# First operand sums on VectorE, first feature stored without its norm, a job clock with other constants, and two buffer slots that change hands, in a decoder-layer kernel

## The chip, the cores and the metric

The kernel runs on one core of a Trainium2 chip. The metric is the device time of one execution in microseconds (us); lower is better. Engines: TensorE (PE, matrix products into PSUM), VectorE (DVE), ScalarE (ACT), GpSimd (POOL) and SyncE (SP, which starts most transfers between HBM and SBUF). Arithmetic is float32; matrix operands are rounded to the fp32r format.

## The reference, cut to what matters

One layer of a hybrid decoder for 1024 prompt tokens and 8 sampled tokens (1032 columns), model width 1024, feed-forward width 2816:

```python
x = x + 0.5 * swiglu(rmsnorm(x, ffn1_norm_g), ffn1_w_in, ffn1_w_out)
mix = token_mix(rmsnorm(x, mix_norm_g), ...)   # window attention (8 heads) and gated DeltaNet (4 heads), then @ w_out_mix
x = x + mix
x = x + 0.5 * swiglu(rmsnorm(x, ffn2_norm_g), ffn2_w_in, ffn2_w_out)
y = rmsnorm(x, final_norm_g)
# swiglu: gate, up = split(x @ w_in); (silu(gate) * up) @ w_out
# rmsnorm: x * rsqrt(mean(x * x) + eps) * g, per token
# DeltaNet per head and chunk of 64 tokens: v_new = u - w @ S; o = qd @ S + qk @ v_new; S = S * gl + kd^T @ v_new
```

## The kernel before

**Products.** Each float32 operand is split into a rounded part (`hi`, ScalarE) and a rest (`lo`, VectorE or GpSimd), and every product is three matmuls: hi·hi, hi·lo, lo·hi (`mm3`, profile lines L325 to L327; `product`, L515 to L517). The columns are cut into three chunks of 344 or into four of 258 (two pairs: p = 0 and 1, l = 0 and 1 within a pair).

**Stages.** First the head of the first FFN: features f = 0 to 3 (`ffn_head`, plain products with operands `xghi`, `xglo`, `phi`, `plo`). Features 4 to 21 are done by a scheme with seven products for eight blocks (`ffn_in`), for which `x_ops` makes seven operands per pair out of four blocks: the sums `t1`, `t2` and two more, and their splits `xhi`, `xlo`; `w_ops` does likewise for the weights. Then `ffn_out`, the mixers (`mix_in`: projections with attention and the DeltaNet scan between them), `mix_out` in two passes, and the second FFN (`ffn_in` from its first feature, and `ffn_out`). In the trace the mixers span about 758 to 1290 us, `mix_out` to 1377.6, the second FFN the rest.

**Norms.** `prepare` does a pair's norm: `squares` adds up the squares, `rstd` sums them over the partitions on TensorE (line L247, output `nv` after a VectorE step), VectorE makes the reciprocal root by ten small instructions on `rsqt` and `rsqy` (`rsqrt`), and scales the identity by it (tile family `t2`, printed `t` in the profile); TensorE spreads that over the partitions by matmuls with `ones` (called the broadcast below: `ps<-t,ones`). Then VectorE scales each 128x258 block `x`, and `x_ops` runs. In the first FFN's head the products take x without its norm, and `evac` multiplies the results in PSUM by `rs`, the broadcast factor, so it must wait for it.

**Order.** The order of TensorE's instructions is the order in which the program issues them. Norms, attention and scan are generators ("jobs"), resumed by `tick` when the program's own clock `now` reaches `job.at`; the clock is a sum of assumed times: `tick` after each triple of matmuls, `book` for every instruction of another engine, `HOP_NS` between two engines. Where a job's small matmuls stand among the products is set by this clock. The other engines' order is chosen by the compiler's scheduler.

**Buffers.** SBUF data lies in 44 slots of 1060 columns. While weights of `ffn_out`, mixers and `mix_out` stream, `WSLOTS` of them belong to the weights: two `raw`, the others `hi`/`lo` pairs. `reserve` and `drop` keep three weights issued. A weight for which no pair is left is loaded to a wide pair of the common slots by `extra`.

## Time and profile before

| | |
|---|---|
| median of 3 runs | 2123.35 us (2121.09 to 2125.12) |
| profiled execution | 2120.43 us, its span 2118.7 us |
| mean granted TensorE clock | 0.962 of full |
| busy time over the span | TensorE 95%, VectorE 56%, ScalarE 32%, GpSimd 28% |

The span runs from the first to the last instruction. A busy TensorE may run at half clock, so its share of busy time says how often it had an instruction, not how fast that went; the granted clock is the other half of that.

### The profile page before, as it was taken

What the parts mean: (1) busy time and instruction counts of PE and PEld (TensorE: products, weight loads), DVE (VectorE), ACT (ScalarE), POOL (GpSimd) and SP (SyncE); (2) the same over time, 40 slices, a digit from 0 to 9 for tenths busy, and PEclk for the clock granted to TensorE, in tenths of its full rate; (3) what the DMA queues carried; (4) which work ended last, traced back from release to release, by engine and by line L of the source; (5) the groups of instructions that cost most, each with busy time, mean ns of one, the idle gap of its engine ahead of it and who ended that gap; (6) DMA issues with size and microseconds to landing.
All of it is one profiled execution on the core that took longest, in us unless ns stands there. A gap on an engine that the chain in (4) does not pass through costs nothing.

```text
span 2118.7 us, 37131 instructions
## 1 busy us (share of the span) xinstructions
PE 2016.0 (95%) x14990; PEld 1964.4 (93%) x14990; DVE 1187.5 (56%) x2634; ACT 673.7 (32%) x1463; POOL 597.4 (28%) x539
## 2 busy tenths in 40 slices
PE   7899999999999999999898988969999999999997
PEld 6899999999999998879788978869999999999997
DVE  7665444446433545786778865775444444464335
ACT  5233323333111324563332422333323333331112
POOL 2544434431000132330211212454444434200003
PEclk8999999999999999998989989979999999999998
DMA  4212222227321221222112261203222222552112
GB/s 149 66 62 94 77 85 72 80 81 283 100 78 51 96 77 45 58 76 64 47 51 54 71 224 57 98 21 99 71 81 81 81 81 79 181 208 78 56 40 81
DMA packets 115293, 187.16 MB, mean 88 GB/s; under 512 B 36080, under 2 KB 67216, under 8 KB 115104
## 3 DMA queue, kind: packets, MB, share of 16 engines
q1 hardware_dynamic: 113360, 178.41, 26.4%
q0 software_dynamic: 1760, 6.37, 0.8%
q8 instruction: 117, 1.92, 0.4%
q14 instruction: 56, 0.46, 0.1%
HBM read 138.77 MB, written 47.02 MB: 88 GB/s over the span
## 4 chain that ended last, share of the span: by engine, by line
PE 77%; DVE 11%; DMA 2%; issue 1%; ACT 1%; SPq 1%; POOL 0%; DVEq 0%; ACTq 0%; POOLq 0%
PE mm L325 11%; PE mm L326 11%; PE mm L327 10%; PE ps L515 9%; PE ps L516 9%; PE ps L517 9%; PE ps L247 5%; PE mm L516 4%; PE mm L515 4%; PE mm L517 4%; DVE conv L89 1%; DVE inv L89 1%; PE ps L252 1%; DVE x L89 1%; DVE xlo L89 1%
## 5 line engine op out<-in xcount | busy, mean ns | idle before, releaser
L515 PE MATMUL ps<-xhi,wop 128*128 128x258 f32 x1600 | 456.2, 285 | 7.0 <-DVE sw L89 2.9
L516 PE MATMUL ps<-xlo,wop 128*128 128x258 f32 x1600 | 454.6, 284 | 5.5 <-DVE xlo L89 5.5
L517 PE MATMUL ps<-xhi,wop 128*128 128x258 f32 x1600 | 454.4, 284 | 0.0
L325 PE MATMUL mm<-hhi,hi 128*128 128x344 f32 x1008 | 322.6, 320 | 0.0
L326 PE MATMUL mm<-hlo,hi 128*128 128x344 f32 x1008 | 322.2, 320 | 0.0
L327 PE MATMUL mm<-hhi,lo 128*128 128x344 f32 x1008 | 322.0, 319 | 0.0
L515 PEld LDWEIGHTS ps<-xhi,wop 128*128 128x128 f32 x1600 | 304.8, 191 | 8.4 <-DVE sw L89 3.7
L516 PEld LDWEIGHTS ps<-xlo,wop 128*128 128x128 f32 x1600 | 305.8, 191 | 6.1 <-DVE xlo L89 6.1
L517 PEld LDWEIGHTS ps<-xhi,wop 128*128 128x128 f32 x1600 | 304.9, 191 | 0.0
L89 DVE TENSOR_TENSOR wop<-r,wop 128x512 fp32r<-128x512 f32 x200 | 156.0, 795 | 196.7 <-ACT wop L89 178.4
L89 DVE SCALAR_TENSOR_TENSOR x<-mm,x 128x344 f32<-128x344 f32 x240 | 123.3, 515 | 220.9 <-PE mm L327 219.5
L516 PE MATMUL mm<-xlo,wop 128*128 128x258 f32 x640 | 182.2, 285 | 9.0 <-DVE xlo L89 9.0
L327 PEld LDWEIGHTS mm<-hhi,lo 128*128 128x128 f32 x1008 | 189.5, 188 | 0.0
L326 PEld LDWEIGHTS mm<-hlo,hi 128*128 128x128 f32 x1008 | 189.4, 188 | 0.0
L325 PEld LDWEIGHTS mm<-hhi,hi 128*128 128x128 f32 x1008 | 189.3, 188 | 0.0
L89 ACT CAST hi<-raw 128x1024 fp32r<-128x1024 f32 (+2 forms) x79 | 76.2, 965 | 336.3 <-PE mm L326 302.6
L515 PE MATMUL mm<-xhi,wop 128*128 128x258 f32 x640 | 182.0, 284 | 0.0
L517 PE MATMUL mm<-xhi,wop 128*128 128x258 f32 x640 | 181.7, 284 | 0.0
L89 POOL TENSOR_TENSOR acc<-acc,t 128x344 f32<-128x344 f32 (+1 forms) x50 | 47.1, 942 | 473.9 <-ACT t L89 464.2
L89 ACT CAST wop<-r 128x512 fp32r<-128x512 f32 x200 | 120.6, 620 | 181.5 <-DMA r<-in_w_in 132.5
L325 PE MATMUL mm<-xnhi,hi 128*128 128x344 f32 x488 | 173.0, 355 | 0.0
L89 POOL TENSOR_TENSOR ws<-r 128x512 f32<-128x512 f32 x40 | 52.3, 1307 | 402.4 <-DMA r<-in_w_in 375.4
(341 smaller groups left out, 4406.1 us busy)
## 6 DMA issues: line engine op xcount, KB each, us to landing
r<-in_w_in SPq DMA_DIRECT2D x86, 512.0 KB, 3.6
hraw<-hd SPq DMA_DIRECT2D x44, 516.0 KB, 4.9
hd<-sw SPq DMA_DIRECT2D x80, 258.0 KB, 2.0
raw<-in_w_out SPq DMA_DIRECT2D x32, 512.0 KB, 3.7
raw<-in_w_mix SPq DMA_DIRECT2D x22, 512.0 KB, 3.7
x<-in_x SPq DMA_DIRECT2D x16, 516.0 KB, 8.9
raw<-in_w_out SPq DMA_DIRECT2D x20, 384.0 KB, 3.2
xd<-x SPq DMA_DIRECT2D x24, 172.0 KB, 1.9
```

What stands on the lines that cost most here:

```text
L89: return fn(out, *a, **k)
L247: self.nc.tensor.matmul(out, lhsT, rhs, start=start, stop=stop, skip_group_check=pair is not None)
L252: self.nc.tensor.transpose(out, x, self.ident[:p, :p])
L325: mm(ps, whi, xhi, start=start, stop=False)
L326: mm(ps, whi, xlo, start=False, stop=False)
L327: mm(ps, wlo, xhi, start=False, stop=stop)
L515: mm(ps, w[:, a], x[0][:, c], start=first, stop=False, skip_group_check=True)
L516: mm(ps, w[:, a], x[1][:, c], start=False, stop=False, skip_group_check=True)
L517: mm(ps, wlo, x[0][:, c], start=False, stop=last, skip_group_check=True)
```

## The change

1. `WSLOTS` goes from 8 to 6, and two weights instead of three are kept issued (`LIVE`); the two slots return to the common ones. In the last group of each `ffn_out` and in `mix_out`'s last pass two weights instead of one go to wide pairs.
2. The job clock's constants are others: longer ways between engines, a short one for two instructions of one job on one engine, other times for triples of matmuls and for small matmuls; a job that yields `None` is resumed up to 1.2 us of its clock ahead of its being ready.
3. The first feature f = 0 leaves PSUM by eight ScalarE copies into two tiles `early`; when all four `rs` blocks are there, two VectorE multiplications of 128x1032, one Silu, one GpSimd multiplication and one transfer do what 8 VectorE, 4 ScalarE and 4 GpSimd instructions and four transfers did.
4. The four sums of `x_ops` and the sum in `squares` move from GpSimd to VectorE, but for the first FFN's pair 1. In all 12 sums of 128x1032 and two adds of squares move.
5. In `mix_out` the eight additions of squares that VectorE had go to GpSimd.

```diff
-WSLOTS = 8
+WSLOTS = 6
+LIVE = 2
...
-PE_NS = 150.0
-HOP_NS = 130.0
+PE_NS = 220.0
+LEAD = 1200.0
+SELF_HOP = 70.0
...
-        self.vector = Timed(net, nc.vector, 70.0, 1.04)
-        self.scalar = Timed(net, nc.scalar, 95.0, 0.83)
-        self.gpsimd = Timed(net, nc.gpsimd, 150.0, 2.1)
+        self.vector = Timed(net, nc.vector, 65.0, 1.05, 260.0)
+        self.scalar = Timed(net, nc.scalar, 185.0, 0.83, 200.0)
+        self.gpsimd = Timed(net, nc.gpsimd, 150.0, 2.1, 260.0)
...
     def book(self, eng, ns, parts):
         cur = self.cur
-        ready = max(cur.ready, self.now + PE_NS)
+        ready = max(cur.last[1] + SELF_HOP if cur.last[0] is eng else cur.ready, self.now + PE_NS)
...
-        cur.ready = end + HOP_NS
+        cur.last = eng, end
+        cur.ready = end + eng.hop
...
                     lat = next(job.gen)
-                    job.at = self.now - lat if lat < 0 else max(job.ready, self.now) + lat
+                    if lat is None:
+                        job.at = max(job.ready - LEAD, self.now)
+                    else:
+                        job.at = self.now - lat if lat < 0 else max(job.ready, self.now) + lat
...
-        self.now += 15.0 if pair else max(110.0, n * 4 / 2.4)
+        self.now += 15.0 if pair else max(222.0 if lhsT.shape[0] == P else 60.0, n * 4 / 2.4)
...
-        for _ in range(3):
+        for _ in range(LIVE):
             self.issue()
...
-        while self.plan and self.live < 3:
+        while self.plan and self.live < LIVE:
             self.issue()
...
-        self.tick(int(xhi.shape[1]) * 3 / 2.36)
+        self.tick(27.0 + int(xhi.shape[1]) * 1.29)
...
-    def x_ops(self, blk, n, out, keep=0):
-
-        tt = self.nc.gpsimd.tensor_tensor
+    def x_ops(self, blk, n, out, keep, eng):
+
+        tt = eng.tensor_tensor
...
-            self.tick(HW * 3 / 2.2)
+            self.tick(27.0 + HW * 1.29)
...
+        def first():
+            while len(done) < 4:
+                yield -300.0
+            for t in early:
+                nc.vector.tensor_tensor(t, t, rs, ALU.mult)
+            nc.scalar.activation(early[0], early[0], AF.Silu)
+            nc.gpsimd.tensor_tensor(early[1], early[1], early[0], ALU.mult)
+            nc.sync.dma_start(hd[:, 0, :], early[1])
+            self.fr(*early)
+            yield PAD
+
+        early = [self.bt(s="early") for _ in range(2)]
...
-                self.due.append((lambda p=p, l=l: (p, l) in done, partial(evac, f, c, *ps)))
-                self.settle_rs(2 if f == 0 else 1)
+                if f:
+                    self.due.append((lambda p=p, l=l: (p, l) in done, partial(evac, f, c, *ps)))
+                    self.settle_rs(1)
+                else:
+                    for t, o in zip(early, ps):
+                        nc.scalar.copy(t[:, c * HW:(c + 1) * HW], o)
...
-                wide = [(self.bt([P, per * g * P], F32R, "whi"), self.bt([P, per * g * P], F32R, "wlo")) for _ in range(KT // per - 3)]
-                ws = [self.take() for _ in range(3)]
+                wide = [(self.bt([P, per * g * P], F32R, "whi"), self.bt([P, per * g * P], F32R, "wlo")) for _ in range(KT // per - LIVE)]
+                ws = [self.take() for _ in range(LIVE)]
...
-            nc.gpsimd.tensor_tensor(a, a, b, ALU.add)
+            eng.tensor_tensor(a, a, b, ALU.add)
...
                 nc.vector.scalar_tensor_tensor(y, y, self.norm_g[:, gi, k:k + 1], bcs[:, :w], ALU.mult, ALU.mult)
+                yield None
...
-            yield -300.0 if ok else -500.0
+            yield None if ok else -500.0
...
-                last = [self.bt([P, per * g * P], F32R, n) for n in ("whi", "wlo")]
-                ws = [self.take() for _ in range(KT // per - 1)]
-                ws.append(self.extra(*last))
+                wide = [(self.bt([P, per * g * P], F32R, "whi"), self.bt([P, per * g * P], F32R, "wlo")) for _ in range(KT // per - LIVE)]
+                ws = [self.take() for _ in range(LIVE)]
+                for t in wide:
+                    ws.append(self.extra(*t))
...
-                        self.square(acc[:, c % 2 * HW:(c % 2 + 1) * HW], m, at(m, c))
+                        self.square(acc[:, c % 2 * HW:(c % 2 + 1) * HW], m, at(m, c), dve=())
...
-            n.spawn(n.prepare(p, xs[p], n.bt(s="acc"), 0, xT[p], rs, done, xg["ready"]))
+            n.spawn(n.prepare(p, xs[p], n.bt(s="acc"), 0, xT[p], (n.nc.vector, n.nc.gpsimd)[p], rs, done, xg["ready"]))
...
-            n.spawn(n.prepare(p, x, acc, 2, xT[p]))
+            n.spawn(n.prepare(p, x, acc, 2, xT[p], n.nc.vector))
```

In TensorE's and VectorE's order this gives the following. Names are those of the program, with numbers.

TensorE in the head of the first FFN, before: the sums of squares of pair 0 (`ps_55`) and its first broadcast (`ps_60`) stand directly behind one another.

```order
L326 MATMUL mm_54_387<-xglo_29_176,phi_10_109 128x258
L327 MATMUL mm_54_387<-xghi_28_175,plo_11_110 128x258
L247 MATMUL ps_55_436<-ones_76,acc_33_180 86x1 x6
L247 MATMUL ps_60_462<-t2_59_458,ones_76 128x86 x3
L325 MATMUL ps_64_486<-xghi_26_173,phi_3_92 128x258
L326 MATMUL ps_64_486<-xglo_27_174,phi_3_92 128x258
```

After, the broadcast (`ps_66`) has 30 product matmuls between itself and the sums; here is where it stands.

```order
L332 MATMUL ps_64_522<-xglo_17_164,phi_38_185 128x258
L333 MATMUL ps_64_522<-xghi_16_163,plo_39_186 128x258
L253 MATMUL ps_66_527<-t2_63_489,ones_76 128x86 x3
L331 MATMUL ps_64_522<-xghi_16_163,phi_38_185 128x258
L332 MATMUL ps_64_522<-xglo_17_164,phi_38_185 128x258
```

Counted in product matmuls from pair 0's first broadcast, pair 1's sums stood 42 behind it, pair 0's second broadcast 48 and pair 1's first 75; after, they stand 81, 84 and 105 behind it, and the last of the three takes the factors `t2_82`.

VectorE at pair 1's norm in the first FFN's head, before: `t2_70` is that broadcast's input, and the two rows ahead of the last are a feature's `evac`, which waits for `rs_32`.

```order
L89 SCALAR_TENSOR_TENSOR x_6_102<-x_6_102,c_norm_g_74,ps_71_562 128x258 x2
L89 SCALAR_TENSOR_TENSOR x_8_106<-x_8_106,c_norm_g_74,ps_71_562 128x258 x4
L89 TENSOR_TENSOR rsqt_69_540<-rsqy_68_539 86x6
L89 SCALAR_TENSOR_TENSOR rsqt_69_540<-rsqt_69_540,nv_67_531 86x6
L89 SCALAR_TENSOR_TENSOR rsqy_68_539<-rsqt_69_540,rsqy_68_539 86x6
L89 TENSOR_SCALAR t2_70_552<-ident_125,rsqy_68_539 86x86 x3
L89 TENSOR_TENSOR t2_76_583<-ps_47_292,rs_32_179 128x258
L89 TENSOR_TENSOR t2_77_584<-mm_48_293,rs_32_179 128x258
L89 TENSOR_SCALAR t2_93_658<-ident_125,rsqy_68_539 86x86 x3
```

The same place after: `t2_82` is the broadcast's input.

```order
L91 SCALAR_TENSOR_TENSOR rsqy_80_655<-rsqt_81_656,rsqy_80_655 86x6
L91 TENSOR_TENSOR t1_89_731<-x_6_102,x_5_100 128x1032
L91 TENSOR_TENSOR rsqt_81_656<-rsqy_80_655 86x6
L91 TENSOR_TENSOR t2_90_732<-x_8_106,t1_89_731 128x1032
L91 TENSOR_TENSOR x_6_102<-x_8_106,x_6_102 128x1032
L91 SCALAR_TENSOR_TENSOR rsqt_81_656<-rsqt_81_656,nv_79_647 86x6
L91 TENSOR_TENSOR xlo_98_793<-t1_89_731,xhi_97_792 128x1032
L91 SCALAR_TENSOR_TENSOR rsqy_80_655<-rsqt_81_656,rsqy_80_655 86x6
L91 TENSOR_TENSOR xlo_101_829<-t2_90_732,xhi_100_828 128x1032
L91 TENSOR_TENSOR xlo_106_867<-x_7_104,xhi_105_866 128x1032
L91 TENSOR_SCALAR t2_82_668<-ident_125,rsqy_80_655 86x86 x3
```

Between the last steps of pair 1's reciprocal root stand now three sums and three rests of pair 0, all 1032 columns wide.

VectorE at the start of the second FFN, before: the last results of `mix_out` (`x_1969`, `acc`), a weight's rest (`wop`) and the rests of the first operands (`xlo`), whose sums `t1`, `t2` come from GpSimd.

```order
L89 TENSOR_TENSOR x_1969_13695<-mm_2136_14732,x_1969_13695 128x258
L89 TENSOR_TENSOR xlo_2144_14759<-x_1966_13689,xhi_2143_14758 128x1032
L89 TENSOR_TENSOR acc_2077_14417<-acc_2077_14417,t2_2131_14708 128x258
L89 TENSOR_TENSOR x_1969_13695<-mm_2142_14754,x_1969_13695 128x258
L89 TENSOR_TENSOR wop_2132_14712<-r1_2110_14600,wop_2132_14712 128x512
L89 TENSOR_TENSOR xlo_2138_14740<-t1_2127_14693,xhi_2137_14739 128x1032
L89 TENSOR_TENSOR xlo_2140_14747<-t2_2128_14694,xhi_2139_14746 128x1032
L89 TENSOR_TENSOR xlo_2148_14775<-x_1967_13691,xhi_2147_14774 128x1032
```

After: pair 0's scalings (the first row and four before it) wait for a broadcast that stands at the very end of `mix_out`, and the sums `t1`, `t2`, `x_1869` and `x_1968` follow on VectorE; pair 1's reciprocal root (`rsqt`, `rsqy`) begins among them.

```order
L91 SCALAR_TENSOR_TENSOR x_1969_13708<-x_1969_13708,c_norm_g_74,ps_2128_14723 128x258 x4
L91 TENSOR_TENSOR t1_2133_14746<-x_1869_13204,x_1868_13202 128x1032
L91 TENSOR_SCALAR nv_2138_14758<-ps_2137_14757 86x6
L91 TENSOR_TENSOR xlo_2156_14892<-x_1969_13708,xhi_2155_14891 128x1032
L91 TENSOR_TENSOR t2_2134_14747<-x_1969_13708,t1_2133_14746 128x1032
L91 TENSOR_SCALAR rsqt_2140_14767<-nv_2138_14758 86x6
L91 TENSOR_TENSOR x_1869_13204<-x_1969_13708,x_1869_13204 128x1032
L91 TENSOR_TENSOR xlo_2145_14796<-t1_2133_14746,xhi_2144_14795 128x1032
L91 TENSOR_TENSOR x_1968_13706<-x_1968_13706,t2_2134_14747 128x1032
L91 TENSOR_SCALAR rsqy_2139_14766<-rsqt_2140_14767 86x6
L91 TENSOR_TENSOR xlo_2148_14819<-t2_2134_14747,xhi_2147_14818 128x1032
```

Counted in product matmuls from the second FFN's first one, TensorE's small matmuls of the norms stand before: pair 0's second broadcast 33 ahead of it, pair 1's sums 129 behind it, both its broadcasts 168 behind. After: pair 0's second broadcast directly ahead, pair 1's sums 3 behind, its broadcasts 24 and 57 behind. In the scan's chain the second matmuls of a step (`ps<-w,kd`) stand mostly 6 product matmuls behind the first (`ps<-R,U`) in the first three heads, as before, and 9 instead of 6 in the last head; from there to the next step's first it is mostly 9 to 12, and was 6 to 12.

## Rows read from the trace of the kernel before

**Rows 1.** Page, part 1: busy time, share of the span and instructions of each engine.

```profile
PE 2016.0 (95%) x14990; PEld 1964.4 (93%) x14990; DVE 1187.5 (56%) x2634; ACT 673.7 (32%) x1463; POOL 597.4 (28%) x539
```

**Rows 2.** Busy time by stage: stretch in us, its length, then for PE, PEld, DVE, ACT and POOL busy us (instructions), the granted TensorE clock as a share of full, the DMA share and GB/s. Stretches: the mixers, mix_out's product, the start of the second FFN, the rest of that FFN.

```profile
758.00:1290.00 532.00, 496.09 (x3561) 451.41 (x3561) 363.91 (x1190) 203.83 (x608) 108.39 (x109) 0.93 0.26 74
1290.00:1377.60 87.60, 77.64 (x610) 76.09 (x609) 59.38 (x129) 30.52 (x67) 32.08 (x30) 0.94 0.24 80
1377.60:1445.00 67.40, 48.19 (x340) 46.53 (x339) 51.87 (x73) 21.69 (x33) 34.44 (x18) 0.80 0.13 39
1445.00:2103.00 658.00, 658.00 (x4990) 657.80 (x4989) 310.12 (x550) 179.12 (x327) 188.79 (x181) 1.00 0.29 93
```

**Rows 3.** PE's instructions in order of time in the first FFN's head, the ones ahead of which PE sat idle: start us, us, engine, line, operation, output<-inputs, tile, count, and in brackets the idle us before it and what ended it.

```profile
23.89 0.58 PE L327 MATMUL mm<-xghi,plo 128*128 128x258 f32 x1 [3.43 <-DVE plo L89]
...
43.86 0.97 PE L247 MATMUL ps<-t,ones 86*128 86x86 f32 x5 [3.24 <-DVE t L89]
...
64.87 0.55 PE L325 MATMUL mm<-xghi,phi 128*128 128x258 f32 x1 [7.75 <-DVE t L89]
```

**Rows 4.** VectorE's instructions in order of time around the last of these waits, same columns.

```profile
53.56 0.16 DVE L89 SCALAR_TENSOR_TENSOR rsqt<-rsqt,nv 86x6 f32<-86x6 f32 x1
...
59.13 2.22 DVE L89 SCALAR_TENSOR_TENSOR rsqy<-rsqt,rsqy 86x6 f32<-86x6 f32 x1
61.38 2.67 DVE L89 TENSOR_SCALAR t<-ident,rsqy 86x86 f32<-86x86 f32 x3
63.98 0.41 DVE L89 TENSOR_TENSOR t<-ps,rs 128x258 f32<-128x258 f32 x1
...
66.31 1.22 DVE L89 TENSOR_TENSOR xlo<-x,xhi 128x1032 fp32r<-128x1032 f32 x1
68.60 3.22 DVE L89 SCALAR_TENSOR_TENSOR x<-x,c_norm_g,ps 128x258 f32<-128x258 f32 x8
```

**Rows 5.** GpSimd's instructions in the same stretch, same columns.

```profile
58.95 2.37 POOL L89 TENSOR_TENSOR t<-x,t 128x1032 f32<-128x1032 f32 x1
```

**Rows 6.** ScalarE's, same columns: a PSUM copy of 128x258 and a rounding of 128x1032.

```profile
67.10 0.38 ACT L89 COPY rs<-ps 128x258 f32<-128x258 f32 x1 [1.25 <-PE ps L247]
67.37 1.06 ACT L89 CAST xhi<-x 128x1032 fp32r<-128x1032 f32 x1
```

**Rows 7.** Busy time by stretch, columns as in rows 2: the long wait of the first FFN's head, what follows it, and the part that follows that.

```profile
57.00:65.00 8.00, 0.24 (x2) 0.17 (x1) 7.90 (x14) 2.52 (x4) 6.59 (x4) 0.77 0.00 1
65.00:72.00 7.00, 7.00 (x35) 7.00 (x36) 7.00 (x14) 2.52 (x4) 6.62 (x2) 0.53 0.05 19
80.00:144.00 64.00, 64.00 (x533) 63.85 (x533) 33.16 (x44) 20.25 (x32) 31.60 (x24) 1.00 0.24 77
```

**Rows 8.** PE's instructions in order of time at the start of the second FFN, the ones that it came to late, columns as in rows 3.

```profile
1384.64 0.58 PE L516 MATMUL mm<-xlo,wop 128*128 128x258 f32 x1 [5.35 <-DVE xlo L89]
...
1391.62 0.39 PE L515 MATMUL ps<-xhi,wop 128*128 128x258 f32 x1 [1.98 <-ACT sw L89]
...
1413.71 0.58 PE L515 MATMUL ps<-xhi,wop 128*128 128x258 f32 x1 [2.17 <-ACT xhi L89]
...
1419.37 0.58 PE L516 MATMUL ps<-xlo,wop 128*128 128x258 f32 x1 [5.08 <-DVE xlo L89]
...
1426.01 0.58 PE L516 MATMUL mm<-xlo,wop 128*128 128x258 f32 x1 [3.69 <-DVE xlo L89]
```

**Rows 9.** VectorE's instructions in order of time in the same stretch.

```profile
1381.19 4.99 DVE L89 TENSOR_TENSOR xlo<-t,xhi 128x1032 fp32r<-128x1032 f32 x2
...
1417.21 5.43 DVE L89 TENSOR_TENSOR xlo<-x,xhi 128x1032 fp32r<-128x1032 f32 x2
1422.57 6.74 DVE L89 TENSOR_TENSOR xlo<-t,xhi 128x1032 fp32r<-128x1032 f32 x2
```

**Rows 10.** GpSimd's, same stretch.

```profile
1376.98 3.74 POOL L89 TENSOR_TENSOR t<-x,t 128x1032 f32<-128x1032 f32 x1
...
1418.30 3.25 POOL L89 TENSOR_TENSOR t<-x,t 128x1032 f32<-128x1032 f32 x1
```

**Rows 11.** Who waited for whom in 750 to 1290 us, the scan's own three of them: engine, line, releaser, us in all, times, longest us.

```profile
PE ps L247 <- ACT w L89: 8.8, 2, 5.6
...
PE ps L247 <- DVE R L89: 3.0, 2, 2.8
...
PE ps L247 <- DVE S L89: 2.3, 4, 0.8
```

**Rows 12.** The longest of these waits: PE's row, and the copy on ScalarE ahead of it.

```profile
1047.37 0.80 PE L247 MATMUL ps<-w,kd 128*128 128x128 f32 x2 [5.63 <-ACT w L89]
...
1044.53 0.64 ACT L89 COPY mg<-mg 128x256 f32<-128x256 f32 x1 [8.52 <-DMA mg<-scr_t]
```

**Rows 13.** A busy stretch of the mixers, columns as in rows 2.

```profile
900.00:950.00 50.00, 45.08 (x305) 35.30 (x305) 42.07 (x128) 31.02 (x92) 16.01 (x23) 1.00 0.31 81
```

**Rows 14.** Groups of instructions by form: line, engine, operation, output<-inputs, tile, count | busy us, mean ns of one | idle us of the engine before them and what ended it.

```profile
L89 ACT CAST hi<-raw 128x1024 fp32r<-128x1024 f32 x52 | 54.5, 1049 | 207.0 <-PE mm L326 178.3 <-DMA raw<-in_w_out 16.4 <-PE ps L326 5.1
L89 POOL TENSOR_TENSOR lo<-raw,hi 128x1024 fp32r<-128x1024 f32 x22 | 52.8, 2398 | 211.0 <-ACT hi L89 174.3 <-PE ps L247 21.2 <-PE mm L327 15.5
L89 ACT CAST hi<-raw 128x768 fp32r<-128x768 f32 x19 | 15.9, 835 | 123.4 <-PE mm L326 123.2 <-issue 0.2
```

**Rows 15.** Page, part 6: output<-input, queue, operation, count, KB each, median us from issue to landing.

```profile
raw<-in_w_out SPq DMA_DIRECT2D x20, 384.0 KB, 3.2
```

More of the change, by code (lines that the diff above doesn't have):

```diff
@@ L73, in __init__ @@
     def __init__(self, gen, at, ready):
-        self.gen, self.at, self.ready = gen, at, ready
+        self.gen, self.at, self.ready, self.last = gen, at, ready, (None, 0.0)
 class Timed:
-    def __init__(self, net, eng, fixed, rate):
-        self.net, self.eng, self.fixed, self.rate, self.free = net, eng, fixed, rate, 0.0
+    def __init__(self, net, eng, fixed, rate, hop):
+        self.net, self.eng, self.fixed, self.rate, self.hop, self.free = net, eng, fixed, rate, hop, 0.0
     def __getattr__(self, name):
@@ L232, in tick @@
         self.cur = self.main
-        self.main.ready = 0.0
+        self.main.ready, self.main.last = 0.0, (None, 0.0)
         self.ticking = False
@@ L346, in rsqrt, with square @@
         return y
-    def square(self, acc, k, x, pool=False):
+    def square(self, acc, k, x, pool=False, dve=DVE_SQ):
         nc = self.nc
@@ L361, in square @@
             nc.scalar.activation(sq, x, AF.Square)
-            (nc.vector if k in DVE_SQ else nc.gpsimd).tensor_tensor(acc, acc, sq, ALU.add)
+            (nc.vector if k in dve else nc.gpsimd).tensor_tensor(acc, acc, sq, ALU.add)
     def rstd(self, acc, cs, use):
@@ L383, in rstd @@
                 self.mmul(bcs[:, o - c0:o - c0 + m], self.ones[:m, :], dgt[:m, i * m:(i + 1) * m])
-            use(bcs, c0, w)
+            more = use(bcs, c0, w)
+            if hasattr(more, "send"):
+                yield from more
     def norm(self, x, gi, c0, w, acc, out):
@@ L634, in ffn_head @@
                 self.adv(2)
+            if f == 0:
+                late = self.spawn(first())
             self.wops[f].clear()
         self.settle_rs(0)
+        self.wait(late)
         self.fr(rs)
@@ L735, in ffn_out @@
                         if c0 + w == TT and m % per == per - 1:
-                            if m // per < 3:
+                            if m // per < LIVE:
                                 self.drop()
@@ L762, in x_blocks, with squares @@
         return xs
-    def squares(self, xs, acc):
+    def squares(self, xs, acc, eng):
         nc = self.nc
@@ L775, in squares, with prepare @@
             self.fr(a, b)
-    def prepare(self, p, xs, acc, gi, out, rs=None, done=None, sq=None):
+    def prepare(self, p, xs, acc, gi, out, eng, rs=None, done=None, sq=None):
         nc = self.nc
@@ L782, in prepare @@
                 yield -300.0
-            yield from self.squares(xs, acc)
+            yield from self.squares(xs, acc, eng)
         def use(bcs, c0, w):
@@ L792, in use @@
                 nc.vector.scalar_tensor_tensor(y, y, self.norm_g[:, gi, k:k + 1], bcs[:, :w], ALU.mult, ALU.mult)
+                yield None
         yield from self.rstd(acc, [(0, HW), (HW, HW)], use)
         self.fr(acc)
-        for ok in self.x_ops([xs[0][0], xs[0][1], xs[1][0], xs[1][1]], 4 * HW, out, 3 if sq is not None else 0):
-            yield -300.0 if ok else -500.0
+        for ok in self.x_ops([xs[0][0], xs[0][1], xs[1][0], xs[1][1]], 4 * HW, out, 3 if sq is not None else 0, eng):
+            yield None if ok else -500.0
     def settle(self, keep):
@@ L1590, in mix_out @@
                         one(m, c, *ws[m // per], js, m % per * g * P)
-                        self.square(acc[:, c % 2 * HW:(c % 2 + 1) * HW], m, at(m, c))
+                        self.square(acc[:, c % 2 * HW:(c % 2 + 1) * HW], m, at(m, c), dve=())
                         if c == 3 and m % per == per - 1:
-                            if m < KT - 1:
+                            if m // per < LIVE:
                                 self.drop()
                             else:
-                                self.fr(*last)
+                                self.fr(*ws[m // per])
                         if c > 1:
```

## The prediction

> **What bounds the kernel now.** First the page's busy time: TensorE 2016.0 us of a span of 2118.7 [rows 1], so 102.7 us are waits of TensorE, and the rest is lost only where its clock is low. Then busy time by stage [rows 2], in which the reader subtracts TensorE's busy time from the length and looks at the clock: 35.9 us of waits in the mixers (532 - 496.09, clock 0.93), 10.0 in `mix_out`, 19.2 at the start of the second FFN (clock 0.80), none in the 658 us behind that at full clock. Then, in order of time, who ended TensorE's waits [rows 3, 8] and what the engine named did just before [rows 4, 5, 9, 10]. Nearly every releaser is VectorE or ScalarE in the chain of a norm or of the scan, so a change of the time has to come from these places: the first FFN's head, the mixers, and the seam between `mix_out` and the second FFN. Away from them TensorE has no gap that another engine could fill.
>
> Prices used throughout. A product matmul of 258 columns at full clock: 64.00 us for 533, 0.120 us. Where the clock stands at 0.53 after a long wait, 35 take 7.00 us, 0.20 each, so such a stretch loses 7.00 - 35 x 0.12 = 2.8 us [rows 7]. A 128x1032 two-operand step on VectorE: 1.22 us, where GpSimd is quiet; eight scalings 3.22; a small step 0.16 and about 0.2 from start to start [rows 4]. The same step on GpSimd: 2.37 [rows 5], up to 3.74 beside VectorE [rows 10].
>
> **The sums on VectorE, second FFN.** Before, 67.4 us hold 340 product matmuls, which need 340 x 0.12 = 40.8: the seam loses 26.6 [rows 2]. The large pieces are 5.35, 1.98, 2.17, 5.08 and 3.69 us of waits [rows 8] plus half clock. They are waits for `xlo`, and `xlo` is slow because GpSimd makes the sums at the same time: two of them take 4.99, 5.43 and 6.74 us [rows 9], against 2 x 1.22 alone, beside GpSimd's sums of 3.74 and 3.25 [rows 10]. After, the order gives this, counted from the moment at which the last broadcast of pair 0 is there, which is also where the first product begins. VectorE: eight scalings 3.22, then `t1`, one `xlo`, `t2`, one more sum and the `xlo` of `t1`, five times 1.22, and two small steps, 0.4: 9.7 us. TensorE has by then the first product, 12 x 0.12 = 1.4, and a stop of some 2.0 for pair 1's sums of squares, whose last additions now run on GpSimd (an estimate: `acc` there waits for up to three additions). So it waits 9.7 - 3.4 = 6.3. The second product takes 1.4, to 11.1; then pair 1's broadcast is in the way, for which VectorE still has four wide steps 4.9, one PSUM step 0.4 [rows 4], eight small 1.6 and the scaled identity 0.6 from three instructions: 9.7 + 7.5 = 17.2, a wait of 6.1, less some 1.0 in which the second product runs at half clock: 5.1. The second broadcast of pair 1 needs eight scalings and two steps more, to about 23, and TensorE, with 33 matmuls to do from 17.2 on, comes at 21.2: some 1.7. The waits sum to 2.0 + 6.3 + 5.1 + 1.7 = 15.1; with one stretch at low clock, 2.8, it is 17.9. Pair 1's operands are then ahead of TensorE, where before they cost 2.17 + 5.08 + 3.69. Gain 26.6 - 17.9 = **8.7 us**; ends: 0, if the new waits are as long as the old, and 16, if the wait for the broadcast and the clock stretch fall away.
>
> The Trainium skill, page "TensorE: Matmul & The Clock Gate", section "HAM oscillation — how this bites in real kernels", says that a kernel that waits between bursts starts each burst cold and pays for it every time, which speaks against an order with waits in a row. By that rule the roughly 60 matmuls up to pair 1's second broadcast would all run at 0.20 instead of 0.12, 4.8 us instead of 2.8, and the gain would be 6.7. The trace agrees as to the stretch behind one long wait [rows 7]; no run here shows the new row of waits yet.
>
> **The head of the first FFN.** Three waits stand there, 3.43, 3.24 and 7.75 [rows 3]. The first is for a weight's rest `plo`, behind sums of squares whose addition leaves GpSimd: 2.37 becomes 1.22, and VectorE is not slowed beside it; I take half of the wait, -1.7 (ends 0 and -3.4). The second is the wait between sums and broadcast of pair 0; 30 product matmuls (3.6 us) now lie between, but a `plo` that waits for its transfer lies in the chain too, so I take -0.2 (ends 0 and -3.2). The third was for an `evac` behind pair 1's reciprocal root, slowed by GpSimd: one small step of 2.22, three of 2.67 instead of 0.6 [rows 4]. That cause is gone, and the first feature's PSUM is freed by ScalarE copies of 0.38 [rows 6] that wait for no norm. But a broadcast of pair 1 now stands 24 matmuls, 2.9 us, behind its sums, and VectorE has to do in between eight scalings 3.22, three sums and three rests 6 x 1.2 = 7.2, the root's small steps 2.0 and the identity 0.6: 13.0. TensorE waits 10.1 in place of 7.75: +2.3. The low clock follows in both. Together +0.4, which I take as **0** (ends -5 and +4). What the eight copies, two wide multiplications and one transfer do afterwards hides behind the head's products, VectorE being busy for 33.16 of 64 us there [rows 7]; without that cover the two would cost 2 x 1.22.
>
> **The mixers.** The constants move the scan's matmuls little in three heads (6 products between its two halves, as before) and from 6 to 9 in the last, with somewhat more between the steps. The scan's own waits are 8.8 + 3.0 + 2.3 = 14.1 us [rows 11]. One of them, 5.63, is of another kind: ScalarE's queue stood behind a copy that waited for a transfer [rows 12], which a longer way does not mend. Of the other 8.5 I take a good half, **-5** (ends: -22, when the queue's wait and half of the remaining 21.8 fall too; +8, when one more such wait and some small ones come in). The low end is not the likely one, since VectorE is busy for 42.07 of 50 us where the waits are dense [rows 13]: what a step waits for is then a queue, not the way between engines.
>
> **Two weights instead of three.** A weight needs ScalarE 1.05 and GpSimd 2.40 [rows 14]. Where a projection runs alone, another weight's products cover that: 72 matmuls of 344 columns at 0.16 (0.12 x 344 / 258) are 11.5 us. Behind the one place where two weights are used together the cover is a third of it, 3.8 against 3.45: nothing. In `mix_out`'s last pass the second wide pair's transfer waits until the first one's split is done, 3.2 [rows 15] and 0.84 [rows 14] and about 0.9 (768 of 1032 columns of 1.22): 4.9 in series; the pass starts on earlier weights, so I take **+1** (ends 0 and 4.9). In `ffn_out` the cover is above 8 us: nothing. The eight additions of squares that go to GpSimd are in the 2.0 above.
>
> **Sum.** -8.7 + 0 - 5 + 1 = -12.7, on the profiled execution's 2120.43: 2107.7. The median of the runs lies 2.9 above that execution, so I name **2109**, about in the middle of 2107.7 and 2110.6.
>
> **The rivals.** (a) The mixers give more: the end of -22 instead of -5, and with the waits the low clock (0.93 over 532 us) partly recovers: about 2090. For it: the constants are of the right kind where a small matmul comes too early. Against it: VectorE's share. (b) No change: VectorE becomes the bound at both seams, 12 sums of 1.22 or 14.6 us in its queue, and the new waits for broadcasts behind them (10.1 and 5.1) eat what is won: 2120. For it: its 51.87 of 67.4 us [rows 2]. Against it: before, it spent much of that beside GpSimd, at twice the price. (c) Slower: the third weight comes late. If two issued weights leave a wait whenever one is dropped, its price is transfer 3.2, 1.05 and 2.40, 6.7, less a cover of 3.8: 2.9 for each. Five such waits (14.5) outweigh the sum, and eight give 2120.4 - 12.7 + 23 = 2131. Against it: the projections' 11.5 us of cover. (d) The mixers lose: two more waits behind a blocked queue at 5.6 each and no gain of 5: 2120.4 - 7.7 + 11 = 2124.
>
> **How the numbers follow.** Forecast 0.42, (a) 0.24, (b) 0.12, (c) 0.11, (d) 0.11. The measurement tells about 0.2%, 4.2 us, from no change: faster means below 2119.1, slower above 2127.6. Forecast and (a) are faster, a part of (b) and (d) too (0.10): 0.76. Same 0.12, slower 0.12. The range 2091 to 2126 reaches to (a) on one side and past (d) on the other and leaves out (c) and the far end of (a). The forecast alone would be 2101 to 2117.
>
> **What would show it.** At the seam: TensorE's waits fall from five large ones to two for `xlo` and a broadcast of about 6 and 5 us, none for pair 1's `xlo`; VectorE's `xlo` there at 1.22. In the head: no wait for `evac`, one of about 10 for a broadcast. In the mixers: waits sum to about 31, with the scan's below 10. Wrong it would be through a new wait for a weight's `lo` in the mixers, a GpSimd queue that holds a `lo`, or a broadcast whose inputs stand deeper in VectorE's queue than counted here.

## The result and the profile after

The changed kernel takes 2128.22 us (median of 20 runs, 2123.76 to 2134.07) against 2122.56 us of the kernel before (20 runs beside it): a ratio of 1.0026, 95% interval 1.0017 to 1.0036. It is slower by some 5.7 us, where 2109 us and a gain were forecast. The profiled execution took 2130.83 us, its span 2129.1, 10.4 us more than the 2118.7 of before; since the medians differ by 5.7 only, some 5 us of that are scatter between executions. One execution each of experiments 8 and 9 was a slow one (9794.74 and 2490.22 us); the ratios leave it out, and without it the medians there are 2127.65 and 2129.43.

The stages, columns as in [rows 2]:

```profile
758.00:1290.00 532.00, 483.32 (x3496) 443.32 (x3495) 359.83 (x1171) 201.19 (x597) 110.17 (x108) 0.91 0.25 73
1290.00:1377.60 87.60, 75.74 (x593) 74.28 (x592) 51.59 (x114) 28.47 (x65) 32.81 (x30) 0.92 0.22 75
1377.60:1445.00 67.40, 51.52 (x377) 49.59 (x376) 52.08 (x101) 24.00 (x37) 14.23 (x15) 0.85 0.14 48
```

The mixers now hold 48.7 us of waits instead of 35.9, `mix_out` 11.9 instead of 10.0, the seam 15.9 instead of 19.2. As later stages have moved, a steadier measure is the moment at which TensorE reaches the same product matmul (both kernels have 13056 of them in the same order; read from TensorE's instructions in order of time). The changed kernel's lead (-) or lag (+), in us, over the kernel before in the profiled executions:

| product matmul | place | changed | sums alone | sums and first feature | old clock | own raw slot |
|---|---|---|---|---|---|---|
| 180 | head, pair 0 | -9.4 | -2.2 | -9.1 | -7.9 | -8.5 |
| 780 | end of head | +0.5 | -8.2 | -12.1 | -11.4 | -10.1 |
| 5700 | first projections | -2.0 | -8.5 | -12.6 | -14.7 | -13.5 |
| 7000 | last head's scan | +0.1 | -1.6 | -6.7 | -16.0 | -14.0 |
| 7060 | behind `ps<-mg,NT` | +18.4 | -1.3 | -8.2 | -16.4 | -15.9 |
| 7480 | last pass | +8.8 | -1.2 | -5.1 | -12.9 | -16.6 |
| 7700 | end of the last pass | +13.5 | -1.4 | -5.0 | -10.1 | -18.5 |
| 7960 | second FFN | +8.0 | -2.4 | -6.4 | -11.4 | -21.3 |
| 13055 | last | +10.3 | -3.4 | -6.0 | -11.3 | -22.0 |

(The last four columns are experiments below.) So the changed kernel gains 9.4 us early in the head and gives it back before the head ends; loses some 11 us at one place in the mixers, of which a lag of 8.8 is left in the last pass; loses 4.7 more by its end in the last pass, wins 5.5 at the seam, and loses 2.3 at the very end. The 18.4 at matmul 7060 overstates the loss in the mixers: 7060 stands behind the wait for `mg` in the changed kernel and ahead of it in the kernel before. At matmul 7200, behind it in both, the lag is 11.1.

A column is one execution, so a few us in it need not come from the change. In the mixers the changed kernel and experiments 1 and 9 have the same small matmuls at the same positions and nearly the same steps on the other engines, and so have the kernel before and experiments 7 and 10. From matmul 5000 to 7250 the first three took 610.8, 610.4 and 619.1 us, the other three 601.9, 609.4 and 609.6: one order differs by 8 to 9 us from execution to execution. The 6.9 us that the sums alone seem to lose between 5700 and 7000 are of this kind (from 960 to 980 us the granted clock was 0.52 in that execution and 0.82 in that of the kernel before). The loss at `mg` stands clear of it: from matmul 7040 to 7200 the first three took 62.3, 59.9 and 62.6 us, the others 50.7, 52.4 and 51.6.

TensorE's rows at these places, the idle time ahead in brackets:

```profile
20.36 0.58 PE L333 MATMUL mm<-xghi,plo 128*128 128x258 f32 x1 [1.35 <-DVE plo L91]
...
48.76 1.55 PE L253 MATMUL ps<-t,ones 86*128 86x86 f32 x6 [5.23 <-DVE t L91]
...
75.31 0.94 PE L253 MATMUL ps<-t,ones 86*128 86x86 f32 x3 [8.66 <-DVE t L91]
...
1254.71 1.06 PE L253 MATMUL ps<-mg,NT 32*32 32x32 f32 x32 [16.63 <-ACT mg L91]
...
1354.97 0.58 PE L333 MATMUL mm<-mhi,wlo 128*128 128x258 f32 x1 [4.68 <-DVE wlo L91]
...
1395.27 0.58 PE L523 MATMUL mm<-xhi,wop 128*128 128x258 f32 x1 [2.03 <-ACT xhi L91]
1398.82 0.58 PE L524 MATMUL mm<-xlo,wop 128*128 128x258 f32 x1 [2.96 <-DVE xlo L91]
...
1405.79 1.55 PE L253 MATMUL ps<-t,ones 86*128 86x86 f32 x6 [4.24 <-DVE t L91]
...
1426.96 0.51 PE L523 MATMUL ps<-xhi,wop 128*128 128x258 f32 x1 [3.23 <-DVE sw L91]
...
2086.59 0.93 PE L253 MATMUL ps<-t,ones 115*128 115x115 f32 x6 [0.85 <-DVE t L91]
...
2104.06 0.92 PE L253 MATMUL ps<-t,ones 115*128 115x115 f32 x6 [0.87 <-DVE t L91]
```

The large one is the last head's `ps<-mg,NT`. `mg` is what `Tb`, the result of the inverse's chain of 62 small VectorE steps, becomes by two transfers through HBM (`scr_t<-Tb`, `mg<-scr_t`). SyncE's queue in order of time and VectorE's steps of that chain (count, then min/median/max ns, first to last start), changed kernel:

```profile
1224.30 15.04 SPq L104 DMA_DIRECT2D x<-xd  x8
...
1241.38 6.72 SPq L104 DMA_DIRECT2D scr_t<-Tb  x4
1250.57 1.81 SPq L104 DMA_DIRECT2D mg<-scr_t  x4
...
L91 DVE TENSOR_TENSOR Tb<-Tb,inv x31: 168/216/1202, 1204.7 to 1238.8; 128x60 f32<-128x60 f32 x3, 128x28 f32<-128x28 f32 x2, 128x54 f32<-128x54 f32 x2, 128x48 f32<-128x48 f32 x2
```

and before, with TensorE's row for `mg` first:

```profile
1250.61 0.69 PE L247 MATMUL ps<-mg,NT 32*32 32x32 f32 x32 [2.55 <-ACT mg L89]
...
1225.71 2.27 SPq L102 DMA_DIRECT2D x<-xd  x2
1228.08 11.81 SPq L102 DMA_DIRECT2D scr_t<-Tb  x4
1239.99 0.60 SPq L102 DMA_DIRECT2D x<-xd  x1
...
1242.50 2.21 SPq L102 DMA_DIRECT2D mg<-scr_t  x4
...
L89 DVE TENSOR_TENSOR Tb<-Tb,inv x31: 166/217/243, 1202.8 to 1227.4; 128x60 f32<-128x60 f32 x3, 128x28 f32<-128x28 f32 x2, 128x54 f32<-128x54 f32 x2, 128x48 f32<-128x48 f32 x2
```

In the changed kernel the chain ends 11.4 us later and eight loads of 516 KB stand in one piece ahead of `scr_t<-Tb`; yet `mg` is there only 4 us later, since before the two transfers were slow too (from 1227.4 to 1249.9). What differs more is TensorE: it reaches `ps<-mg,NT` at 1238.1 instead of 1248.1, because the order has it 42 product matmuls earlier (7044 behind the start, was 7086).

### The profile page after: what moved, and what is told of

It reads as the page before. It is cut to its first block, busy times and chain, and to the rows that moved or that the text cites. A ratio compares the mean times of both kernels' runs of the same rounds, so it can differ in the third digit from the quotient of the medians.

```text
span 2129.1 us, 37080 instructions
## 1 busy us (share of the span) xinstructions
PE 2011.0 (94%) x14990; PEld 1963.6 (92%) x14990; DVE 1185.8 (56%) x2634; ACT 677.7 (32%) x1468; POOL 566.8 (27%) x530
## 4 chain that ended last, share of the span: by engine, by line
PE 81%; DVE 11%; DMA 3%; SPq 2%; issue 1%; ACT 1%; POOL 0%; DVEq 0%; ACTq 0%; POOLq 0%
PE mm L331 12%; PE mm L333 11%; PE mm L332 11%; PE ps L523 9%; PE ps L525 9%; PE ps L524 9%; PE ps L253 5%; PE mm L523 3%; PE mm L525 3%; PE mm L524 3%; DVE conv L91 2%; SPq L104 2%; DVE x L91 1%; PE ps L258 1%; DVE inv L91 1%
## 5 line engine op out<-in xcount | busy, mean ns | idle before, releaser
L331 PE MATMUL mm<-hhi,hi 128*128 128x344 f32 x960 | 307.0, 320 | 0.0
L333 PE MATMUL mm<-hhi,lo 128*128 128x344 f32 x960 | 306.7, 320 | 0.0
L332 PE MATMUL mm<-hlo,hi 128*128 128x344 f32 x960 | 306.6, 319 | 0.0
L333 PEld LDWEIGHTS mm<-hhi,lo 128*128 128x128 f32 x960 | 180.4, 188 | 0.0
L332 PEld LDWEIGHTS mm<-hlo,hi 128*128 128x128 f32 x960 | 180.4, 188 | 0.0
L331 PEld LDWEIGHTS mm<-hhi,hi 128*128 128x128 f32 x960 | 180.3, 188 | 0.0
L91 POOL TENSOR_TENSOR acc<-acc,t 128x344 f32<-128x344 f32 (+1 forms) x58 | 52.7, 908 | 475.5 <-ACT t L91 472.2
L91 DVE TENSOR_TENSOR sw<-ps,sw 128x258 f32<-128x258 f32 x240 | 101.1, 424 | 121.8 <-PE ps L525 120.5
```

The lines of the kernel that those rows point to most:

```text
L91: return fn(out, *a, **k)
L331: mm(ps, whi, xhi, start=start, stop=False)
L332: mm(ps, whi, xlo, start=False, stop=False)
L333: mm(ps, wlo, xhi, start=False, stop=stop)
```

## The experiments

Times are medians; ratios are to the kernel before, on the same chip, with 95% intervals.

**1. The loads of x on another queue.**

```diff
-  self.nc.sync.dma_start(b.rearrange(...), get(kh, c0))      # mix_out's x_blocks
+  self.tc.nc.gpsimd.dma_start(b.rearrange(...), get(kh, c0))
```

> The changed kernel, but the eight loads of x for mix_out (x<-xd) are issued from GpSimd's queue instead of SyncE's. Theory A (SyncE's queue: the eight loads stand ahead of the last head's scr_t<-Tb and mg<-scr_t and hold them up): the 16.6 us wait of TensorE for mg shrinks below 6 us, time 8 to 13 us below the changed kernel, about 2116 to 2120 us. Theory B (the transfers themselves crowd the DMA engines, whoever issues them): the wait for mg stays above 11 us, time within 4 us of the changed kernel.

2127.12 us, 1.0032 (1.0018 to 1.0045): theory B, in the time and, just, in the wait for `mg`, 11.6 instead of 16.6 us. Of the 5.0 us between them only 2.0 are won: TensorE goes on from `ps<-mg,NT` at 1252.7 instead of 1254.7, and has come to it at 1241.1 instead of 1238.1. In this run the chain still ends at 1240.9.

**2 and 3. The slots, both ways.**

```diff
-WSLOTS = 6          # e2: the changed kernel     e3: the kernel before, 8 -> 6 and 3 -> 2
-LIVE = 2
+WSLOTS = 8
+LIVE = 3
```

> The changed kernel with 8 weight slots and three live weights again. Theory A (two more common slots let mix_out's x loads be issued early and together): the wait for mg falls from 16.6 us to below 10, and the wait of 4.7 us for the second wide pair's wlo in mix_out's last pass disappears: 8 to 14 us faster than the changed kernel, 2114 to 2120 us. Theory B (the other positions of the scan, not the slots, put them together): the wait for mg stays above 13 us, only the 4.7 go: about 2123 us.

2131.99 us, 1.0054 (1.0040 to 1.0068). The waits for `mg` (4.5) and `wlo` (none) go as theory A says, and the time still rises, as the lag builds up earlier in the mixers (+14.6 at matmul 7000, where the changed kernel has +0.1). So with the new clock nothing is won by giving the slots back.

> The kernel before with 6 weight slots and two live weights, nothing else changed. Theory A (slots alone make the two waits): a wait for mg well above the 2.6 us of before, a new wait for wlo of about 4 us in mix_out's last pass, 8 to 18 us slower than before, 2130 to 2140 us. Theory B (slots alone only cost the wide pair): 3 to 6 us slower.

2123.03 us, 1.0018 (1.0003 to 1.0034): some 3.8 us slower, theory B's price. The wait for `mg` is 6.6, that for `wlo` 4.4; the other waits in the mixers are as long as before in sum (33.2 after 33.4).

**4. The clock's constants alone.**

```diff
+LEAD, SELF_HOP, PE_NS 220, hops 260/200/260, tick and mmul as changed; yields as before
```

> The kernel before with the job clock's new constants (without the jobs that yield None), nothing else changed. Forecast's step: mixers 5 us faster, nothing elsewhere: about 2118 us. Rival 1: the constants bring nothing in the mixers, waits there stay at 35 to 37 us: 2121 to 2125 us. Rival 2: they cost 2 us in the last norm (a broadcast that comes too early, as in the changed kernel's 2085 and 2103 us waits) and more in the mixers: above 2126 us.

2146.48 us, 1.0125 (1.0103 to 1.0147): 26 us slower, rival 2 and more. Its profiled execution, 2138.52 us, was the fastest of the six, so that its profile shows 18 of the 26: 6.6 us are lost in the head, about 10 in the mixers, 2.2 in the last norm.

**5. SELF_HOP.**

```diff
-SELF_HOP = 70.0
+SELF_HOP = 130.0
```

> The changed kernel with SELF_HOP 130 instead of 70. Theory (the clock counts a step of a chain on one engine as 65 + 70 + its length, where the trace shows about 0.2 us from start to start for the reciprocal root and 0.26 for the inverse, so the matmuls behind such chains are placed too early): the waits for the last norm's broadcasts (0.85 and 0.87) vanish, the 16.6 us wait for mg falls below 10, 4 to 12 us faster than the changed kernel, 2112 to 2122. Rival (the longer ways between engines and the slower ticks cost, not the short one): the time stays within 3 us of the changed kernel, 2123 to 2129.

2116.87 us, 0.9972 (0.9956 to 0.9987): one constant is worth 11.5 us, (1.0026 - 0.9972) x 2121, and turns the loss into a gain. The last norm's waits are gone, as expected. The wait for `mg` is not: 13.8 us. The chain now ends at 1227.4 as before, but seven loads of x stand ahead of `scr_t<-Tb` on SyncE's queue, to 1236.8. So the theory has the time right, and is wrong about `mg`.

**6. The changed kernel with the clock of before** (constants and yields).

> The changed kernel with the job clock of before (constants and yields); slots, sums and first feature as changed. Theory (the constants cost what the rest wins): head and seam keep their gain, the tail's 2.2 us go, the mixers are as in the run with slots alone: about 4 to 10 us faster than before, 2110 to 2116. Rival (sums and first feature win only with the new positions): within 3 us of the run with slots alone, 2121 to 2126.

2108.47 us, 0.9945 (0.9926 to 0.9964). The theory holds, a little beyond its range: the clock costs (1.0026 - 0.9945) x 2121 = 17 us of a change whose other parts win 12.

**7. Sums and first feature alone** (with the additions of squares on GpSimd; slots and clock of before).

> The kernel before with the sums on VectorE, the first feature stored without its norm and the additions of squares on GpSimd; slots and job clock as before. Theory: the forecast's seam and head without the clock's cost, and without the 4.4 us wait for the second wide pair: 8 to 14 us faster than before, 2106 to 2112. Rival (the old positions of the broadcasts hide the gain): 0 to 4 us faster, 2116 to 2121.

2110.36 us, 0.9947 (0.9928 to 0.9966). The theory's time, but not its places: in the profile 12.1 us are won in the head, and at the seam (matmuls 7700 to 7960) 1.4.

**8. Ticks alone** (`tick` and `mmul` as changed, in the kernel before).

> The kernel before with the new times of triples and small matmuls alone (tick and mmul), the times of the other engines as before. Theory (SELF_HOP and the ways between engines place matmuls too early in long chains): ticks alone cost little, 2118 to 2126. Rival (ticks are the cause of the clock's 26 us: a clock that runs faster per matmul gives every job fewer matmuls of cover): 2130 or more.

2127.83 us, 1.0032 (1.0015 to 1.0049): 7 us slower, just beyond the theory's range and short of the rival's. Ticks cost something, the times of the other engines more.

**9. The yields of before, constants as changed.**

```diff
-                yield None
...
-            yield None if ok else -500.0
+            yield -300.0 if ok else -500.0
```

> The changed kernel with the jobs' yields as before (a step every 0.3 us of the clock, none that yields None), all constants as changed. Theory (the yields cause pair 1's broadcast 24 matmuls behind its sums, the constants pair 0's 30 behind): the wait of 8.7 us for pair 1's broadcast goes, pair 0's of about 5 stays; about 5 to 9 us faster than the changed kernel, 2118 to 2122. Rival (constants alone make both): within 3 us of the changed kernel.

2131.15 us, 1.0046 (1.0030 to 1.0062): no faster than the changed kernel, where 5 to 9 us were expected. As to positions the theory is right (pair 1's broadcast 69 matmuls behind its sums instead of 24, its wait 1.8 instead of 8.7; pair 0's still 30, 4.8 us); but the 8.9 us of lead at matmul 180 are down to 4.1 at the head's end, two waits for a weight having come in (2.06 for `phi`, 1.25 for `plo`), and the seam wins 3.9 instead of 5.5. What this profile loses beyond that in the mixers is not TensorE's order, which is there that of the changed kernel.

**10. The sums alone** (the kernel before, sums on VectorE).

> The kernel before with the sums on VectorE alone: first feature, additions of squares, slots and clock as before. With the run of sums and first feature together (11 us faster than before) it splits the gain. Theory (the head's gain comes from the first feature, whose PSUM no longer waits for a norm): 0 to 4 us faster than before, with the 7.75 us wait for an evac still there in some size. Rival (the sums alone free VectorE from GpSimd): 8 us faster or more.

2112.55 us, 0.9959 (0.9948 to 0.9971): the rival. TensorE's large waits around pair 0's and pair 1's norm, which were 3.24 and 7.75 [rows 3], and VectorE's steps of pair 1's root with the sum `t` behind it:

```profile
41.04 0.87 PE L247 MATMUL ps<-t,ones 86*128 86x86 f32 x6 [2.81 <-DVE t L89]
55.42 0.87 PE L247 MATMUL ps<-t,ones 86*128 86x86 f32 x6 [2.15 <-DVE x L89]
...
50.93 0.16 DVE L89 SCALAR_TENSOR_TENSOR rsqt<-rsqt,nv 86x6 f32<-86x6 f32 x1
51.13 0.16 DVE L89 SCALAR_TENSOR_TENSOR rsqy<-rsqt,rsqy 86x6 f32<-86x6 f32 x1
...
51.91 0.60 DVE L89 TENSOR_SCALAR t<-ident,rsqy 86x86 f32<-86x86 f32 x3
...
55.53 0.41 DVE L89 TENSOR_TENSOR t<-mm,rs 128x258 f32<-128x258 f32 x1
...
56.38 1.22 DVE L89 TENSOR_TENSOR t<-x,x 128x1032 f32<-128x1032 f32 x1
```

Here the root's steps take 0.16 again (before, one took 2.22 and three of the scaled identity 2.67 [rows 4]), the `evac` that TensorE waited for is done at 55.9 instead of 64.7, and the sums stand behind it.

**11. A raw slot of its own for the second wide pair**, with the clock of before.

```diff
-  ws.append(self.extra(*t))
+  ws.append(self.extra(*t, self.bt([P, per * g * P], s="raw") if i else None))   # extra: use it, free it after the split
```

> The changed kernel with the clock of before, and the second wide pair's raw weight in a common slot of its own, so that its transfer needn't wait for the first one's split. Theory (the 4.4 us wait for wlo hangs on that transfer): no wait for wlo in mix_out's last pass, 3 to 5 us faster than the run with the old clock (2108.5): 2103 to 2106. Rival (the wait is given back at the seam, where VectorE is late anyway): within 2 us of that run.

2098.69 us, 0.9898 (0.9877 to 0.9919): 10 us faster than the run with the old clock, two to three times what was expected, and 22 us faster than before. Who waited for whom there (1245 to 1362 us), first in the run with the old clock, then here:

```profile
PE ps L254 <- ACT t L90: 5.1, 1, 5.1
PE mm L329 <- DVE wlo L90: 4.4, 1, 4.4
PE mm L327 <- DVE x L90: 1.3, 1, 1.3
```

```profile
PE mm L327 <- DVE x L90: 3.0, 3, 1.3
PE ps L254 <- ACT t L90: 1.2, 1, 1.2
PE mm L329 <- DVE lo L90: 1.0, 1, 1.0
```

The wait for `wlo` is gone; a wait of 5.1 us in the last head's output norm went with it (to 1.2). That norm's reciprocal root is again a chain of small VectorE steps. With the old clock GpSimd makes sums for the second FFN's weights (`ws`, `r`) beside it, and five of the steps take 1.12 to 1.46 us:

```profile
1289.34 1.29 POOL L90 TENSOR_TENSOR r<-r,r 128x512 f32<-128x512 f32 x1
1290.59 1.78 POOL L90 TENSOR_TENSOR r<-r,ws 128x512 f32<-128x512 f32 x1
...
1289.43 1.22 DVE L90 SCALAR_TENSOR_TENSOR rsqt<-rsqt,onv 128x4 f32<-128x4 f32 x1
...
1291.17 1.22 DVE L90 SCALAR_TENSOR_TENSOR rsqy<-rsqt,rsqy 128x4 f32<-128x4 f32 x1
```

Here these sums begin behind a transfer, when the root is done but for its last step, and no step takes over 0.17:

```profile
1292.45 1.28 POOL L90 TENSOR_TENSOR ws<-r 128x512 f32<-128x512 f32 x1 [5.95 <-DMA r<-in_w_in]
...
1291.33 0.16 DVE L90 SCALAR_TENSOR_TENSOR rsqt<-rsqt,onv 128x4 f32<-128x4 f32 x1
1291.52 0.16 DVE L90 SCALAR_TENSOR_TENSOR rsqy<-rsqt,rsqy 128x4 f32<-128x4 f32 x1
```

That second part was not foreseen, and no run isolates it. The kernel before has it too (five steps of 1.11 to 1.46 us, and a wait of 5.58 behind them).

**12. Yields of before and SELF_HOP 130.**

> The changed kernel with the yields of before and SELF_HOP 130, other constants as changed. Theory (yields and the short way on one engine are most of the clock's cost): 2110 to 2117. Rival (ticks and the times of small matmuls cost as much): 2118 to 2124.

2113.27 us, 0.9968 (0.9950 to 0.9986): with either kind of yields SELF_HOP is the larger part: from 1.0026 to 0.9972 with the changed yields, from 1.0046 to 0.9968 with the old ones. The remaining distance to the run with the old clock, 5 us, is left to the other constants, by subtraction.

**13. SELF_HOP 130 and the loads of x on GpSimd's queue.**

> The changed kernel with SELF_HOP 130 and the eight loads of x for mix_out on GpSimd's queue. Theory (two things hold mg up side by side: VectorE's chain of the inverse, which ends 11 us later than before, and SyncE's queue with the eight loads; each alone left 11.6 and 13.8 us): together the wait for mg falls to 3 to 7 us, 8 to 10 us less than in the run with SELF_HOP 130 alone, about 2107 to 2113 us. Rival (a third thing holds it, such as the transfers' own landing): the wait stays above 10 us, 2114 to 2118 us.

2116.24 us, 0.9975 (0.9961 to 0.9989). The rival: the wait for `mg` is 17.2 us. VectorE's chain ends at 1225.9 and SyncE's queue is free, but the transfers take their time themselves:

```profile
1225.88 17.92 SPq L104 DMA_DIRECT2D scr_t<-Tb  x4
1246.26 1.82 SPq L104 DMA_DIRECT2D mg<-scr_t  x4
...
1210.00:1250.00 40.00, 21.85 (x158) 21.01 (x156) 20.86 (x77) 10.21 (x31) 15.63 (x22) 0.83 0.92 289
```

The last row is the stretch's busy time: the DMA engines are busy for 0.92 of it at 289 GB/s; before it was the same (0.92, 294 GB/s). Ten loads of `m` and eight of x, 516 KB each, stand around the end of the chain in every version, and no run moves them away, so that `mg` did not come much sooner in any. What differs is where TensorE's matmul stands. Position of `ps<-mg,NT` in product matmuls, and the wait:

| run | position | wait, us |
|---|---|---|
| changed; loads on GpSimd; old yields | 7044 | 16.6; 11.6; 15.5 |
| SELF_HOP 130; with old yields; with loads on GpSimd | 7059 | 13.8; 13.7; 17.2 |
| ticks alone | 7065 | 3.7, after 9.3 for loads of `m` |
| slots back; clock alone | 7077 | 4.5; 4.7, after 6.7 and 6.0 for loads of `m` |
| before; sums alone; sums and first feature | 7086 | 2.5; 3.1; 4.0 |
| slots alone; old clock; own raw slot | 7098 | 6.6; 5.9; 5.5 |

Position is not all: at 7098 the wait is longer than at 7086. And no run moves this matmul alone.

## Why the prediction was wrong

**The mixers (forecast -5): wrong, and the main error.** The step that failed is "The constants move the scan's matmuls little", with the gain of a good half of 8.5 us that was taken for it. The scan's own waits did not fall: 10.9 us for `R`, 2.2 for `w` and 1.4 for `S`, 14.5 after 14.1 [rows 11]. And a term was missing: the wait for `mg`, 16.63 after 2.55 us, which costs some 10 us (matmuls 7040 to 7200 above). The step counted the scan's distances, and did not follow the matmuls that stand behind long chains on one engine or behind transfers. There two of the new constants put matmuls earlier.

The first is SELF_HOP. With 70 the clock counts a small VectorE step of 50 columns as 65 + 52 + 70 = 187 ns, where the old clock counted 70 + 52 + 130 = 252; a root's step of 6 columns is 141 now and was 206. The trace has 0.20 us from start to start in an undisturbed root, and in the inverse before a median of 0.25 and, with what comes between, (1227.4 - 1202.8) / 60 = 0.41. So the old constant was about right and the new one is too short; over 62 steps that is 4 us of cover less. With 130 the matmul stands 15 positions later (experiment 5). The second is the tick. A triple of 344 columns counts 471 ns, as the trace has it (0.47), where the old clock counted 437, so a delay of the clock is now covered by fewer matmuls; ticks alone put the matmul 21 positions earlier (experiment 8). Neither clock knows how long the two transfers take: `scr_t` and `mg` took 22.5 us before (1227.4 to 1249.9).

Experiments 4, 5, 6 and 12 show the cost of the clock; the place of some 10 of its 17 us is read from the traces, where 42 to 54 matmuls decide at `mg`. That slots and new clock together put it at 7044, where each alone puts it at 7077 or 7098, is measured but not explained.

**The head (forecast 0): the number held, and what it hid was missed.** The measured +0.5 is near, and the waits came about as forecast: `plo` 1.35 (half of 3.43), pair 0's broadcast 5.23 (3.0), pair 1's 8.66 (10.1), none for an `evac`. But the sums alone win 8.2 us there, and 12.1 with the first feature. The forecast had the cause of the 7.75 us wait right (small VectorE steps of 2.22 and 2.67 us beside GpSimd's sums) and set against it the new waits, worked out from the order with the new clock. Those are the clock's work, not the sums': with the old clock pair 0's broadcast stands 66 matmuls behind its sums instead of 30 and TensorE does not wait for it, and pair 1's 42 instead of 24 (wait 4.9). Taken part by part the term would have read -12 and +12.

**The seam (forecast -8.7): right in sign, 5.5 measured.** `xlo` (2.96 instead of 6.3) and the broadcast (4.24 instead of 5.1) were shorter than forecast; two waits had no place in the sum, for `xhi` (2.03) and for PSUM results `sw` that VectorE takes out too late (1.12 and 3.2), its queue being full of scalings, sums and rests. The low clock lasted longer than the one stretch of the sum: 0.50 from 1396 to 1400 us and 0.58 from there to 1412. The sum also took all 340 TensorE instructions of the stage before for product matmuls; 313 are. With the old clock the seam gives only 1.0 to 2.8, so here the new positions do help, and they come from the yields: with those of before experiments 9 and 12 win 3.9 and 2.4 there, with the changed ones experiments 1, 2, 5 and 13 win 5.4 to 8.1.

**Two weights (forecast +1, end 4.9): near the upper end, by another cause.** The last pass loses 4.7 us, of which the wait for the second wide pair is 4.68. That it equals the 4.9 in series is luck. The pass comes to that pair 54 matmuls, some 7 us, after its start. Its transfer was issued at 1345.09, when an earlier split had freed the `raw` slot, and `whi` was done at 1349.7; then `wlo` stood 4.0 us behind two results `x` and rests of the second FFN's weights (`wop`) in VectorE's queue, where the sum had VectorE free:

```profile
1348.99 2.57 DVE L91 TENSOR_TENSOR wop<-r,wop 128x512 fp32r<-128x512 f32 x2
...
1351.82 1.70 DVE L91 TENSOR_TENSOR wop<-ws,wop 128x512 fp32r<-128x512 f32 x1
...
1353.77 1.15 DVE L91 TENSOR_TENSOR wlo<-raw,whi 128x768 fp32r<-128x768 f32 x1
```

**The last norm (no term).** Two broadcasts come too early, 0.85 and 0.87 us, and 2.3 us are lost there; with SELF_HOP 130 they are gone (experiment 5).

**Rivals.** (d), the mixers lose behind a blocked queue, was the nearest in its cause, at 2124 and a chance of 0.11; the queue was a crowded DMA stretch, and there was one wait of 16.6, not two of 5.6. (c) has the nearest time, 2131, but a late weight happened once, not five times, and behind VectorE's queue. (b), no change, has the wrong reason: where the clock is the old one, the sums on VectorE win.

## What to carry to other kernels

When a change alters a clock by which a program places work, a constant that is nearer to the trace can still make things worse: the ticks are, and alone they cost 7 us, since there are delays that the clock does not know (queues shared with other jobs, transfers in a crowded stretch) and, as far as the traces tell, a matmul placed later had covered them. Another constant was moved away from the trace, and that cost 11.5: compare each with the time from start to start. Forecast such a change by the positions of the matmuls that end the longest chains, each against the time at which its data can be there, not by the typical distance. And price each part against the old order as well as the new: here two parts of 12 us each cancelled within 0.5 us in one stage.

## What was not expected of the hardware

Small VectorE steps with two SBUF inputs beside a GpSimd sum of 2.4 us took up to 2.22 instead of 0.16 us [rows 4, 5]; moving three of four sets of sums away was worth 8.7 us (1 - 0.9959 = 0.0041 of 2121). The Trainium skill, page "SBUF — State Buffer", section "Who interferes with whom", says that a VectorE instruction with two SBUF inputs contends with a GpSimd instruction that reads SBUF, and that the port pair which they share is an exclusive lock; experiments 10 and 11 agree, with 0.16 us for such a step where GpSimd is quiet and up to 1.46 in the last head's norm where it is not. And four transfers of a small tile took 17.9 us on the queue while the DMA engines moved 289 GB/s, with the large loads on GpSimd's queue (experiment 13), and 11.8 before, with those of x on SyncE's.
